# The front of an RWKV-7 / mLSTM / PEER layer: rewritten RWKV preparation, stores issued from ScalarE, w_out interleaved with the merge

## The chip, the cores and the metric

One core of one Trainium2 chip runs the whole layer in one launch. The metric is device time in microseconds (us). PE is the matrix engine (TensorE), DVE is VectorE, ACT is ScalarE, POOL is GpSimd, SP is SyncE, which here does nothing but issue DMAs.

## The reference

One layer on 512 tokens of width 1024, in float32:

```
h = rmsnorm(x);  z = h @ w_in                 # 1024 x 5896
y_rw = rwkv7(z[:, :1792])                     # 8 heads of 64
    zs = z + (z_prev - z) * mu                # token shift, 14 columns of 128
    kk = k*k_k / max(sqrt(sum(k*k_k)^2 per head), 1e-12)
    S = S*w + (S @ -kk) (kk*a)^T + v k^T ;  y = S @ r      # recurrence over tokens
y_ml = mlstm(z[:, 1792:3848])                 # 4 heads of 128, conv of 4 taps
gate = sigmoid(z[:, 3848:] + gate_b)          # two gates of 1024
merged = gate0 * (y_rw @ p_rw) + gate1 * (y_ml @ p_ml)
x1 = x + merged @ w_out
out = rmsnorm(x1 + peer(rmsnorm(x1)))         # product-key experts
```

## The kernel before

All large products are made exact to about float32 by splitting each operand into a high and a low part: `split` (L97 to L99) has ACT copy the high part and DVE or POOL subtract it to get the low part, and `mm3` (L92 to L95) then issues three matmuls (L93, L94, L95) where one would do. A "column" is a block of 128 of w_in's outputs for all 512 tokens: one 512 KB load, one split (`wh` on ACT, `wl` on DVE), 24 matmuls of 128x512 into a PSUM tile `m`. There are 46 columns and one for the mLSTM gates.

The front runs in stages. (1) Prologue: x is normalised in four blocks of 128 tokens (`norm`, L111 to L119: a square with a sum, a reciprocal root, a scaling), transposed on PE (L127) and split into `hh`, `hl`; the first two columns go ahead in halves (`cols2`). (2) Preparation: `shifted` makes the token shift of a column (POOL subtract L217, DVE combine L218); `prep(i)` (L268 to L353) makes for each pair of heads the decay, the normalised key `kk`, the scaled tensors, and three groups of PE work: a norm (L288), the bonus sum (L324, over `rx`), four transposed tensors (L337, copied by ACT at L339 and stored by SP) and 32 small products (L349, L350). (3) Inverse: 31 steps of a DVE multiply and reduce (L393, L395) invert 32x32 blocks for all chunks. (4) Solve: the recurrence over four blocks of 128 tokens (L412 to L521), a chain PE, ACT, DVE, PE. The mLSTM heads (`mhead`) and the remaining columns (`mcol` stores z to `dz`, `gate` stores to `dgate`) fill the gaps of PE. (5) Merge (L640 to L727): 8 "m" branches and 8 "r" branches of 12 matmuls each, then `half(b, 0, ...)`, the first half of w_out for four token blocks, 24 matmuls each. `branch` multiplies the product by the gate on DVE (L680); in an r branch POOL adds the m part (L694) and `split` makes `mh`, `ml`, which w_out needs for all d. (6) From the second half of w_out on (the tile `o`): norm2, the query projection and the PEER experts.

The engines each run their instructions in the order they stand. The order in the front is worked out by the framework's scheduler from the program and the pools' buffer counts; a list F says how many columns are put between the pieces. From (6) on the order is written by hand and every engine's instructions there stand in the same order in both kernels. SP's queue holds the loads and the stores in one row: a store that waits for its producer keeps the loads behind it.

Of the kernel before, what the change touches and what calls it, by code (L numbers as in the profile page):

```python
# [73 lines left out]
def hybrid_block(ctx: ExitStack, tc: tile.TileContext, A, out, dbg=None):  # L74
# [64 lines left out]
    with ExitStack() as fr:  # L139
# [16 lines left out]
        with ExitStack() as st:  # L156
            xp = pool(st, "xp", 2)
            for b in range(TB):
                xt = xp.tile([128, D], FT, name="xt", bufs=4)
                nc.sync.dma_start(xt, A["x"][b * 128:(b + 1) * 128, :])  # L160
                if b == 0:
                    nc.sync.dma_start(ident, A["ident"])
                    nc.sync.dma_start(vec, A["vec"])
                xs = norm(xp, xt)
                transposed(xp, sm, xs, "norm1_g", hh, hl, b, (b % 2,))

        def wtile(src, n, sub=None):
            w = wr.tile([128, KD, n], FT, name="wf")
            nc.sync.dma_start(w, src)
            h = wr.tile([128, KD, n], FR, name="wh")  # L170
            l = wr.tile([128, KD, n], FR, name="wl")
            split(w, h, l, sub)
            return h, l

# [11 lines left out]
        def cols2(j0):  # L186

            ws = [wtile(A["w_in_t"][j], 128, nc.gpsimd) for j in (j0, j0 + 1)]
# [11 lines left out]
        first = cols2(12)  # L200
# [7 lines left out]
        zwa = tmp.tile([128, T], FT, name="zwa")  # L208
        def shifted(j, dst, ps=None):
# [22 lines left out]
        def gate(j):  # L232
# [3 lines left out]
            nc.sync.dma_start(dgate[j], t)  # L236
# [5 lines left out]
        def mcol(n):  # L242
# [4 lines left out]
            nc.sync.dma_start(dz[4 * j + h], t)  # L247
# [24 lines left out]
        def prep(i):  # L272
# [30 lines left out]
            nc.gpsimd.tensor_tensor(L, L, sg, op=OP.subtract)  # L303
# [10 lines left out]
            nc.gpsimd.tensor_tensor(bh, kk, aa, op=OP.mult)  # L314
# [16 lines left out]
            nc.gpsimd.tensor_tensor(v8(bp), v8(bh), pcb, op=OP.mult)  # L331
            nc.gpsimd.tensor_tensor(v8(kp), v8(kh), pcb, op=OP.mult)
            for n, src in enumerate((vx, None, bp, kp)):
# [6 lines left out]
                nc.sync.dma_start(dX[:, :, n, i * 128:(i + 1) * 128].rearrange("b p c -> p b c"), tt)  # L340
# [303 lines left out]
    mp = pool(me, "mp1", 1, side="right", reuse_waits="tile")  # L644
    mf = [mp.tile([128, T], FT, name=f"mf{d}") for d in range(KD)]
    ysm = [mp.tile([128, 4, T], FR, name="ym" + x) for x in "hl"]
    mt = pool(me, "mt", 2, side="right", reuse_waits="tile")
# [34 lines left out]

    todo = [("m", A["p_ml_t"][d], 8 + d) for d in range(KD)] + [("r", A["p_rw_t"][d], d) for d in range(KD)]
    ahead = [weights(*todo.pop(0))]
    load_y("m", dym)
    for d in range(2 * KD):
# [11 lines left out]

    def wo_tiles(c, his, los):

        for k in range(KD):
            w = mt.tile([128, 512], FT, name="wo", bufs=2)
            nc.sync.dma_start(w, A["w_out"][k * 128:(k + 1) * 128, c * 512:(c + 1) * 512])
            split(w, his[k], los[k])
        return list(zip(his, los))

    def half(b, c, wo, ps, part):

        sl, cs = slice(b * 128, (b + 1) * 128), slice(c * 512, (c + 1) * 512)
        for k in range(KD):  # L710
            mm3(ps, mh[:, k, sl], ml[:, k, sl], wo[k][0], wo[k][1], k == 0, k == KD - 1)
        nc.vector.tensor_tensor(xts[b][:, cs], xts[b][:, cs], ps, op=OP.add)
        sc = mt.tile([128, 512], FT, name="sc", tag="pg", bufs=3)
        nc.scalar.activation(sc, xts[b][:, cs], AF.Square, accum_out=part)

    sq = [[mq.tile([128, 1], FT, name=f"sq{b}{c}") for c in range(2)] for b in range(TB)]
    wo = wo_tiles(0, [m3.tile([128, 512], FR, name=f"woh{k}") for k in range(KD)],
                  [m3.tile([128, 512], FR, name=f"wol{k}") for k in range(KD)])
    for b in range(TB):
        nc.sync.dma_start(xts[b], A["x"][b * 128:(b + 1) * 128, :])  # L720
        half(b, 0, wo, mm.tile([128, T], FT, name="m"), sq[b][0])
    wl = [mp.tile([128, 4, 512], FR, name=f"wol1{n}", tag="ym" + "hl"[n]) for n in range(2)]
    wo = wo_tiles(1, [mp.tile([128, 512], FR, name=f"woh1{k}", tag=f"mf{k}") for k in range(KD)],
                  [wl[k // 4][:, k % 4] for k in range(KD)])
    me2.close()

# [87 lines left out]
    transposed(mt, rps, xs[3], "norm2_g", th, tl, 3)  # L814
# [547 lines left out]
```

## Time and profile before

| what | us |
|---|---|
| median of 3 runs | 1925.1 (1921.32 to 1927.17) |
| the profiled execution, its own time | 1927.14 |
| span of its trace | 1925.4 |
| prologue, 0 to 40.2 | PE busy 21.39 |
| preparation, 40.2 to 236.3 | PE busy 177.55 of 196.10 |
| inverse, 236.3 to 305.7 | PE busy 62.23 of 69.40 |
| solve, 305.7 to 479.8 | PE busy 172.85 of 174.10 |
| merge, 479.8 to 565.9 | PE busy 73.19 of 86.10 |
| the rest, 565.9 to the end | PE busy 1312.19 of 1359.50 |

The span is cut at the first and last matmuls of the stages. Busy is the sum of the time in which an engine had an instruction running; PEclk in a row is the clock that TensorE was granted, as a share of 2.4 GHz.

### The profile page before, as it was taken

How to read it: one execution, taken by the hardware profiler on the slowest of the kernel's cores; microseconds unless marked ns; L12 is line 12 of the kernel's file. 1: busy time of each engine (PE TensorE's matmuls, PEld its weight loads, DVE VectorE, ACT ScalarE, POOL GpSimd, SP SyncE). 2: the span in 40 equal slices, each digit the busy share in tenths (PEclk: the TensorE clock that was granted, in tenths of full speed). 3: DMA queues.
4: the chain of work that ended last, by engine and by line, in shares of the span. 5: the costliest groups of instructions: out<-in, count | busy, mean ns of one | idle time of the engine just before them, and what ended most of it. 6: DMA issues, size and time to landing. Idle time of an engine off the chain costs nothing.

```text
span 1925.4 us, 27329 instructions
## 1 busy us (share of the span) xinstructions
PE 1819.4 (94%) x10241; PEld 1593.6 (83%) x10241; DVE 1386.7 (72%) x2516; ACT 743.0 (39%) x1099; POOL 619.3 (32%) x538
## 2 busy tenths in 40 slices
PE   6888999999889998998999999999999999999998
PEld 5666777888668988897999977799999999998786
DVE  4568693544634599989888556777788878787975
ACT  4346432654434333323444433333333333333433
POOL 2421102110123555453222211144554444443400
PEclk8989999999999999998999999999999999999999
DMA  3244645432834344344888988989999999998982
GB/s 141 83 139 156 170 154 199 146 107 88 280 112 151 123 162 153 110 160 140 269 265 266 290 289 276 309 299 319 327 330 314 337 312 338 314 328 274 370 279 84
DMA packets 242499, 431.37 MB, mean 224 GB/s; under 512 B 22976, under 2 KB 149568, under 8 KB 241344
## 3 DMA queue, kind: packets, MB, share of 16 engines
q1 hardware_dynamic: 156144, 270.24, 42.2%
q0 software_dynamic: 36864, 134.23, 20.1%
q10 hardware_dynamic: 49360, 25.17, 4.7%
q8 instruction: 80, 1.31, 0.3%
q14 instruction: 51, 0.42, 0.1%
HBM read 372.83 MB, written 56.75 MB: 223 GB/s over the span
## 4 chain that ended last, share of the span: by engine, by line
PE 67%; DVE 17%; DMA 7%; issue 4%; ACT 3%; POOL 2%; SPq 0%; DVEq 0%; ACTq 0%; POOLq 0%
PE h L93 7%; PE h L94 7%; PE h L95 7%; PE po L93 7%; PE po L94 7%; PE po L95 7%; PE w L1163 5%; PE m L95 3%; PE m L93 3%; DMA as<-dA 3%; PE m L94 3%; DVE wl L99 1%; DVE vl L99 1%; DMA vf<-in_v_dram 1%; DVE ge L1006 1%
## 5 line engine op out<-in xcount | busy, mean ns | idle before, releaser
L93 PE MATMUL h<-tl,wh 128*128 128x384 f32 x1024 | 350.8, 343 | 0.0
L95 PE MATMUL h<-th,wl 128*128 128x384 f32 x1024 | 347.3, 339 | 3.2 <-POOL wl L99 3.2
L94 PE MATMUL h<-th,wh 128*128 128x384 f32 x1024 | 347.2, 339 | 0.0
L859 POOL DMA_INDIRECT gat<-in_u_dram,eid x128 | 176.1, 1376 | 404.1 <-DVE gat L864 387.5
L93 PE MATMUL po<-vl,ah 128*128 128x512 f32 x654 | 258.8, 396 | 14.7 <-DVE vl L99 14.5
L94 PE MATMUL po<-vh,ah 128*128 128x512 f32 x654 | 257.5, 394 | 0.0
L95 PE MATMUL po<-vh,al 128*128 128x512 f32 x654 | 257.2, 393 | 0.0
L98 ACT ACTIVATE wh<-wf 128x1024 fp32r<-128x1024 f32 x208 | 218.6, 1053 | 90.8 <-PE m L94 58.5
L859 POOL DMA_INDIRECT gat<-in_v_dram,eid x128 | 180.8, 1412 | 215.8 <-DVE acc L870 190.2
L99 DVE TENSOR_TENSOR vl<-vf,vh 128x1024 fp32r<-128x1024 f32 x111 | 135.9, 1224 | 131.0 <-ACT vh L98 130.8
L99 DVE TENSOR_TENSOR wl<-wf,wh 128x1024 fp32r<-128x1024 f32 x152 | 188.0, 1237 | 50.7 <-ACT wh L98 48.7
L854 ACT ACTIVATE act<-h 128x384 f32<-128x384 f32 x98 | 48.2, 492 | 429.9 <-PE h L95 429.9
L95 PEld LDWEIGHTS h<-th,wl 128*128 128x128 f32 x1024 | 195.4, 191 | 3.5 <-POOL wl L99 3.5
L93 PEld LDWEIGHTS h<-tl,wh 128*128 128x128 f32 x1024 | 196.3, 192 | 2.4
L94 PEld LDWEIGHTS h<-th,wh 128*128 128x128 f32 x1024 | 195.8, 191 | 2.3
L99 POOL TENSOR_TENSOR wl<-wf,wh 128x1024 fp32r<-128x1024 f32 x56 | 136.5, 2448 | 142.8 <-ACT wh L98 140.3
L870 DVE SCALAR_TENSOR_TENSOR acc<-gat,dots,acc 128x1024 f32<-128x1024 f32 x128 | 164.0, 1281 | 2.4
L864 DVE SCALAR_TENSOR_TENSOR gat<-gat,tok 128x1024 f32<-128x1024 f32 x128 | 159.2, 1267 | 4.0 <-DMA gat<-in_u_dram,eid 4.0
L93 PE MATMUL m<-hl,wh 128*128 128x512 f32 (+1 forms) x392 | 155.1, 396 | 5.6 <-ACT wh L98 5.6
L95 PE MATMUL m<-hh,wl 128*128 128x512 f32 (+1 forms) x392 | 154.9, 395 | 5.1 <-DVE wl L99 4.9
L93 PEld LDWEIGHTS po<-vl,ah 128*128 128x128 f32 x654 | 124.5, 190 | 41.8 <-ACT ah L98 17.2
L94 PE MATMUL m<-hh,wh 128*128 128x512 f32 (+1 forms) x392 | 153.9, 393 | 0.0
(384 smaller groups left out, 3344.4 us busy)
## 6 DMA issues: line engine op xcount, KB each, us to landing
wf<-in_u_t_dram SPq DMA_DIRECT2D x128, 512.0 KB
vf<-in_v_dram SPq DMA_DIRECT2D x111, 512.0 KB
W<-dW SPq DMA_DIRECT2D x32, 768.0 KB
wf<-in_w_in_t_dram SPq DMA_DIRECT2D x46, 512.0 KB
dW<-stg ACTq DMA_DIRECT2D x11, 2048.0 KB
wf<-in_v_dram SPq DMA_DIRECT2D x17, 512.0 KB
wf<-in_w_q_t_dram SPq DMA_DIRECT2D x16, 512.0 KB
dA<-as SPq DMA_DIRECT2D x30, 192.0 KB
```

What stands on the lines that cost most here:

```text
L93: nc.tensor.matmul(ps, lh, rl, start=first, stop=False)
L94: nc.tensor.matmul(ps, lh, rh, start=False, stop=False)
L95: nc.tensor.matmul(ps, ll, rh, start=False, stop=last)
L98: nc.scalar.activation(hi, src, AF.Copy)
L99: (sub or nc.vector).tensor_tensor(lo, src, hi.bitcast(FT), op=OP.subtract)
L854: nc.scalar.activation(act[i], ps, AF.Gelu)
L859: nc.gpsimd.indirect_dma_start(out=t, out_offset=None, in_=src, in_offset=bass.IndirectOffsetOnAxis(ap=eid[:, j:j + 1], axis=0))
L864: nc.vector.scalar_tensor_tensor(t, t, 1.0, tok0, op0=OP.mult, op1=OP.mult, accum_out=dots[:, j:j + 1])
L870: nc.vector.scalar_tensor_tensor(acc, t, dots[:, j:j + 1], acc, op0=OP.mult, op1=OP.add)
L1006: nc.vector.tensor_tensor(ge, x.rearrange("p b (a r) -> p (b a) r", r=4).unsqueeze(2).to_broadcast(big), rank.unsqueeze(1).to_broadcast(bi ...
L1163: nc.tensor.matmul(ps[:, r], og[k][:, a, :, r], O1[:, a, :, r], start=k == 0, stop=k == 1)
```

## The change

1. Prologue: the square with its sum goes from ACT to DVE; the four x loads and the loads of the first two weight tiles are issued together, x0 and x1 before the weights, x2 and x3 behind them; all low parts are made by DVE.
2. `shifted`: z*(1-mu) is made by ACT, DVE adds z_prev*mu. POOL's subtract goes.
3. `prep`: the sum of squares is made by four matmuls with the tokens on the partitions (2 columns each), so that the root, the reciprocal and the Newton step work on 128x8 instead of 128x512; the result is spread out to 128x512 and put back by four PE transposes (L310 of the changed kernel). L-sg, bh, bp and kp go from POOL to DVE.
4. The stores of `dgate`, `dz` and `dX` (16 each) are issued from ACT's queue.
5. Merge: weights are fetched two branches ahead; x and the w_out tiles are loaded and split within the loop over the r branches, four tiles deep instead of two; the first half of w_out is computed tile by tile (`first_half(k)`: 12 matmuls, tile k for four token blocks) two r branches behind the branch that made its input, into four PSUM tiles of their own.

```diff
-        nc.scalar.activation(xs, xt, AF.Square, accum_out=ss)
+        nc.vector.scalar_tensor_tensor(xs, xt, 1.0, xt, op0=OP.mult, op1=OP.mult, accum_out=ss)
...
-            d = tmp.tile([128, T], FT, name="zd", bufs=2)
-            nc.gpsimd.tensor_tensor(d, z[:, 0:T], z[:, 1:], op=OP.subtract)
-            nc.vector.scalar_tensor_tensor(dst, d, V("rw_mu", j), z[:, 1:], op0=OP.mult, op1=OP.add)
+            nc.scalar.activation(dst, z[:, 1:], AF.Identity, scale=omu[:, j:j + 1])
+            nc.vector.scalar_tensor_tensor(dst, z[:, 0:T], V("rw_mu", j), dst, op0=OP.mult, op1=OP.add)
...
-            nc.sync.dma_start(dgate[j], t)
+            nc.scalar.dma_start(dgate[j], t)
...
-            ps = sm.tile([128, T], FT, name="s")
-            nc.tensor.matmul(ps, C("bdones"), q, start=True, stop=True)
-            nc.scalar.activation(q, ps, AF.Sqrt)
-            nc.vector.tensor_scalar(q, q, 1e-19, None, op0=OP.max)
-            nc.vector.reciprocal(q, q)
+            ps = sm.tile([128, TB, 2], FT, name="s")
+            for tb in range(TB):
+                nc.tensor.matmul(ps[:, tb], q[:, tb * 128:(tb + 1) * 128], C("bdones")[:, 0:128:64], start=True, stop=True)
+            n2 = tmp.tile([128, TB, 2], FT, name="n2", bufs=2)
+            nc.vector.tensor_copy(n2, ps)
+            iv = tmp.tile([128, TB, 2], FT, name="iv", bufs=2)
+            nc.scalar.activation(iv, n2, AF.Sqrt)
+            nc.vector.tensor_scalar(iv, iv, 1e-19, None, op0=OP.max)
+            nc.vector.reciprocal(iv, iv)
+            nc.vector.scalar_tensor_tensor(n2, iv, -0.5, n2, op0=OP.mult, op1=OP.mult)
+            nc.vector.tensor_tensor(n2, n2, iv, op=OP.mult)
+            nc.vector.scalar_tensor_tensor(iv, n2, 1.5, iv, op0=OP.add, op1=OP.mult)
+            ivb = tmp.tile([128, TB, 2, 64], FT, name="ivb")
+            nc.vector.tensor_scalar(ivb, iv.unsqueeze(3).to_broadcast([128, TB, 2, 64]), 1e12, None, op0=OP.min)
+            ps = sm.tile([128, TB, 128], FT, name="s")
+            for tb in range(TB):
+                nc.tensor.transpose(ps[:, tb], ivb[:, tb], ident)
+            nc.vector.tensor_tensor(kk, kk, ps.rearrange("p b t -> p (b t)"), op=OP.mult)
             L = tmp.tile([128, T], FT, name="L")
-            nc.vector.scalar_tensor_tensor(L, q, -0.5, ps, op0=OP.mult, op1=OP.mult)
-            nc.gpsimd.tensor_tensor(L, L, q, op=OP.mult)
-            nc.vector.scalar_tensor_tensor(q, L, 1.5, q, op0=OP.add, op1=OP.mult)
-            nc.vector.scalar_tensor_tensor(kk, q, 1e12, kk, op0=OP.min, op1=OP.mult)
...
-            nc.gpsimd.tensor_tensor(bh, kk, aa, op=OP.mult)
+            nc.vector.tensor_tensor(bh, kk, aa, op=OP.mult)
...
+    def first_half(k):
+
+        for b in range(TB):
+            sl = slice(b * 128, (b + 1) * 128)
+            mm3(pso[b], mh[:, k, sl], ml[:, k, sl], wo[k][0], wo[k][1], k == 0, k == KD - 1)
+
     todo = [("m", A["p_ml_t"][d], 8 + d) for d in range(KD)] + [("r", A["p_rw_t"][d], d) for d in range(KD)]
-    ahead = [weights(*todo.pop(0))]
+    LAG = 2
     load_y("m", dym)
+    ahead = [weights(*todo.pop(0)), weights(*todo.pop(0))]
...
+            wo.append(wo_tile(0, d, m3.tile([128, 512], FR, name=f"woh{d}"), m3.tile([128, 512], FR, name=f"wol{d}")))
+            if d < TB:
+                nc.sync.dma_start(xts[d], A["x"][d * 128:(d + 1) * 128, :])
+            if d >= LAG:
+                first_half(d - LAG)
+    for k in range(KD - LAG, KD):
+        first_half(k)
```

How instructions move, in three places. First DVE in the preparation of the first pair of heads, ahead of the bonus sum's input `rx`; before:

```order
L310 TENSOR_TENSOR KR<-rx,ei 128x512
L315 TENSOR_TENSOR bh<-bh,en 128x512
L320 TENSOR_TENSOR kh<-kx,en 128x512
L322 SCALAR_TENSOR_TENSOR rx<-rx,vec,kx 128x512
L309 TENSOR_TENSOR KR<-kk,L 128x512
```

and in the changed kernel, where L338 makes `rx` and L311 waits for the four transposes:

```order
L307 TENSOR_SCALAR ivb<-iv 128x512
L323 COPY PC<-ei 128x8
L326 TENSOR_TENSOR KR<-rx,ei 128x512
L311 TENSOR_TENSOR kk<-kk,s 128x512
L319 TENSOR_TENSOR L<-L,sg 128x512
L330 TENSOR_TENSOR bh<-kk,aa 128x512
L99 TENSOR_TENSOR wl<-wf,wh 128x1024
L325 TENSOR_TENSOR KR<-kk,L 128x512
L331 TENSOR_TENSOR bh<-bh,en 128x512
L333 TENSOR_SCALAR aa<-aa,vec 128x512
L347 TENSOR_TENSOR bp<-bh,PC 128x512
L334 SCALAR_TENSOR_TENSOR kx<-aa,kx 128x512
```

L-sg, bh and bp now stand in DVE's row; `rx` follows two rows later.

Second SP's queue where the merge's loads begin (`yl` loads the mLSTM's output, `pw` a branch's weights, `pg` its gate); before:

```order
L236 DMA dgate_360<-ze_4016 128x512
L667 DMA pw_4104<-in_p_ml_t_dram 128x512
L669 DMA pg_4106<-dgate_360 128x512
L662 DMA yl_4112<-dym_63 128x512
L662 DMA yl_4116<-dym_63 128x512
L662 DMA yl_4120<-dym_63 128x512
L236 DMA dgate_360<-ze_4050 128x512
L662 DMA yl_4124<-dym_63 128x512
```

and after:

```order
L636 DMA dym_63<-so_3283 128x512
L158 DMA wf_4059<-in_w_in_t_dram 128x1024
L679 DMA yl_4159<-dym_63 128x512
L537 DMA dyr_62<-ya_3711 512x1x128
L679 DMA yl_4163<-dym_63 128x512
L679 DMA yl_4167<-dym_63 128x512
L679 DMA yl_4171<-dym_63 128x512
L686 DMA pg_4177<-dgate_360 128x512
```

The gate stores have left the row (they stand in ACT's), and the `yl` loads stand ahead of the weights and the gates.

Third PE where the third r branch ends; in the changed kernel the first w_out tile follows (`wo0` to `wo3` are the four PSUM tiles), and then the fourth r branch:

```order
L95 MATMUL m_4455<-yrh_4139,pwl_4388 128x512
L93 MATMUL wo0_4155<-wol0_4409,mh_4118 128x512
L94 MATMUL wo0_4155<-woh0_4408,mh_4118 128x512
L95 MATMUL wo0_4155<-woh0_4408,ml_4119 128x512
L93 MATMUL wo1_4156<-wol0_4409,mh_4118 128x512
L94 MATMUL wo1_4156<-woh0_4408,mh_4118 128x512
L95 MATMUL wo1_4156<-woh0_4408,ml_4119 128x512
```

Before, the first matmul on `mh` stood behind the last r branch:

```order
L94 MATMUL m_4495<-yrh_4099,pwh_4474 128x512
L95 MATMUL m_4495<-yrh_4099,pwl_4475 128x512
L93 MATMUL m_4569<-wol0_4528,mh_4094 128x512
L94 MATMUL m_4569<-woh0_4520,mh_4094 128x512
L95 MATMUL m_4569<-woh0_4520,ml_4095 128x512
```

Twelve matmuls of w_out now stand between two r branches from the third on, and 24 behind the last.

## Rows read from the trace of the kernel before

**Rows 1.** Windows by stage: start:end, us, each engine's busy us, PEclk, DMA share, GB/s

```profile
0.00:40.20 40.20, 21.39 (x128) 20.38 (x129) 20.31 (x37) 15.62 (x26) 12.14 (x16) 0.87 0.40 142
40.20:236.30 196.10, 177.55 (x943) 135.41 (x942) 131.16 (x154) 99.99 (x133) 53.93 (x52) 0.96 0.46 139
236.30:305.70 69.40, 62.23 (x260) 49.08 (x259) 58.12 (x86) 22.77 (x27) 6.91 (x11) 0.98 0.51 172
305.70:479.80 174.10, 172.85 (x1721) 145.56 (x1721) 77.42 (x172) 83.46 (x134) 20.14 (x26) 1.00 0.37 122
479.80:565.90 86.10, 73.19 (x289) 55.99 (x289) 46.08 (x67) 31.51 (x55) 12.82 (x9) 0.94 0.62 202
565.90:1925.40 1359.50, 1312.19 (x6906) 1187.22 (x6904) 1053.60 (x2001) 489.62 (x724) 513.33 (x425) 0.98 0.76 256
```

**Rows 2.** Waits of PE from 0 to 580: total us, times, longest

```profile
PE s L324 <- DVE rx L322: 16.2, 4, 5.7
PE s L127 <- DVE xs L118: 14.7, 2, 12.5
...
PE m L93 <- ACT mh L98: 5.6, 2, 3.1
...
PE m L93 <- DVE yml L99: 3.9, 2, 3.6
```

**Rows 3.** Timeline of DVE, prologue: start, us, instruction

```profile
20.70 2.08 DVE L107 TENSOR_TENSOR rsq<-rs 128x1 f32<-128x1 f32 x1
```

**Rows 4.** Page, costliest groups: count, busy us, mean ns

```profile
L99 DVE TENSOR_TENSOR wl<-wf,wh 128x1024 fp32r<-128x1024 f32 x152 | 188.0, 1237 | 50.7 <-ACT wh L98 48.7
...
L864 DVE SCALAR_TENSOR_TENSOR gat<-gat,tok 128x1024 f32<-128x1024 f32 x128 | 159.2, 1267 | 4.0 <-DMA gat<-in_u_dram,eid 4.0
```

**Rows 5.** Timeline of DVE, first preparation

```profile
77.97 3.35 DVE L291 RECIPROCAL q<-q 128x512 f32<-128x512 f32 x1
...
84.36 1.52 DVE L295 SCALAR_TENSOR_TENSOR q<-L,q 128x512 f32<-128x512 f32 x1 [1.18 <-POOL L L294]
...
88.86 0.49 DVE L317 TENSOR_SCALAR aa<-aa,vec 128x512 f32<-128x512 f32 x1 [1.12 <-POOL bh L314]
...
93.19 0.68 DVE L320 TENSOR_TENSOR kh<-kx,en 128x512 f32<-128x512 f32 x1
93.80 1.52 DVE L322 SCALAR_TENSOR_TENSOR rx<-rx,vec,kx 128x512 f32<-128x512 f32 x1
```

**Rows 6.** Timeline of PE, first preparation

```profile
95.38 2.08 PE L324 MATMUL s<-rx,cst 128*128 128x512 f32 x2 [5.67 <-DVE rx L322]
```

**Rows 7.** Windows of two stretches with the lower granted clock

```profile
94.16:100.98 6.82, 5.61 (x20) 4.14 (x22) 6.16 (x7) 1.19 (x2) 2.26 (x4) 0.50 0.27 77
...
544.71:551.54 6.83, 5.24 (x12) 4.13 (x13) 2.60 (x5) 3.13 (x6) 1.07 (x2) 0.50 0.36 111
```

**Rows 8.** Timeline of PE, merge

```profile
508.90 0.39 PE L93 MATMUL m<-yml,pwh 128*128 128x512 f32 x1
509.13 0.40 PE L94 MATMUL m<-ymh,pwh 128*128 128x512 f32 x1
...
546.30 0.80 PE L93 MATMUL m<-wol,mh 128*128 128x512 f32 x1 [3.08 <-ACT mh L98]
```

**Rows 9.** Timeline of POOL, merge

```profile
535.96 1.61 POOL L694 TENSOR_TENSOR pg<-pg,mf 128x512 f32<-128x512 f32 x1 [2.13 <-DVE pg L680]
539.70 1.58 POOL L694 TENSOR_TENSOR pg<-pg,mf 128x512 f32<-128x512 f32 x1 [2.13 <-DVE pg L680]
```

**Rows 10.** Transfers from 479 to 520: packets, MB, mean GB/s

```profile
DMA packets 6241, 11.82 MB, mean 288 GB/s; under 512 B 690, under 2 KB 690, under 8 KB 6238
```

**Rows 11.** Timeline of SP's queue, start of the merge

```profile
481.33 0.32 SPq L236 DMA_DIRECT2D dgate<-ze  x1
481.74 0.38 SPq L662 DMA_DIRECT2D yl<-dym  x1
```

**Rows 12.** Stores issued from ACT: ns min/median/max

```profile
L1169 ACTq DMA_DIRECT2D dW<-stg x13: 366/366/868, 914.1 to 1089.5; - x13
```

More of the change, by code (lines that the diff above doesn't have):

```diff
@@ L155, in hybrid_block @@
         hl = io.tile([128, KD, T], FR, name="hl")
[L156 to L165, printed above, removed]
         def wtile(src, n, sub=None):
@@ L173, in wtile @@
             return h, l
+        with ExitStack() as st:
+            xp = pool(st, "xp", 2)
+            xt = []
+            for b in range(TB):
+                xt.append(xp.tile([128, D], FT, name="xt", bufs=4))
+                nc.sync.dma_start(xt[b], A["x"][b * 128:(b + 1) * 128, :])
+                if b == 0:
+                    nc.sync.dma_start(ident, A["ident"])
+                if b == 1:
+                    nc.sync.dma_start(vec, A["vec"])
+                    ws12 = [wtile(A["w_in_t"][j], 128) for j in (12, 13)]
+            for b in range(TB):
+                xs = norm(xp, xt[b])
+                transposed(xp, sm, xs, "norm1_g", hh, hl, b)
         def col(j):
@@ L184, in colw, with cols2 @@
             return ps
-        def cols2(j0):
-            ws = [wtile(A["w_in_t"][j], 128, nc.gpsimd) for j in (j0, j0 + 1)]
+        def cols2(ws):
             ps = [mm.tile([128, T], FT, name="m") for _ in range(2)]
@@ L199, in hybrid_block @@
         zg = rw.tile([128, T], FT, name="zg")
-        first = cols2(12)
+        first = cols2(ws12)
         nc.sync.dma_start(cst, A["cst"])
@@ L208, in hybrid_block @@
         zwa = tmp.tile([128, T], FT, name="zwa")
+        omu = tmp.tile([128, 14], FT, name="omu")
+        o_mu = VEC["rw_mu"][0]
+        nc.vector.tensor_scalar(omu, vec[:, o_mu:o_mu + 14], -1.0, 1.0, op0=OP.mult, op1=OP.add)
         def shifted(j, dst, ps=None):
@@ L643, in hybrid_block @@
     me = ExitStack()
[L644 to L647, printed above, removed]
     mq = pool(me, "mp", 1, side="right", reuse_waits="tile")
@@ L651, in hybrid_block @@
     ml = mq.tile([128, KD, T], FR, name="ml")
+    mp = pool(me, "mp1", 1, side="right", reuse_waits="tile")
+    ysm = [mp.tile([128, 4, T], FR, name="ym" + x) for x in "hl"]
+    mt = pool(me, "mt", 2, side="right", reuse_waits="tile")
+    mf = [mp.tile([128, T], FT, name=f"mf{d}") for d in range(KD)]
     me2 = ExitStack()
@@ L655, in hybrid_block @@
     mm = pool(me2, "mm2", 4, space=PSUM, reuse_waits="tile")
+    wps = pool(me2, "wo2", 1, space=PSUM, reuse_waits="tile")
     ys = {}
@@ L681, in branch, with wo_tile, residual, half @@
         return dst
+    def wo_tile(c, k, hi, lo):
+        w = mt.tile([128, 512], FT, name="wo", bufs=4)
+        nc.sync.dma_start(w, A["w_out"][k * 128:(k + 1) * 128, c * 512:(c + 1) * 512])
+        split(w, hi, lo)
+        return hi, lo
+    def residual(b, c, ps, part):
+        cs = slice(c * 512, (c + 1) * 512)
+        nc.vector.tensor_tensor(xts[b][:, cs], xts[b][:, cs], ps, op=OP.add)
+        sc = mt.tile([128, 512], FT, name="sc", tag="pg", bufs=3)
+        nc.scalar.activation(sc, xts[b][:, cs], AF.Square, accum_out=part)
+    def half(b, c, wo, ps, part):
+        sl = slice(b * 128, (b + 1) * 128)
+        for k in range(KD):
+            mm3(ps, mh[:, k, sl], ml[:, k, sl], wo[k][0], wo[k][1], k == 0, k == KD - 1)
+        residual(b, c, ps, part)
+    sq = [[mq.tile([128, 1], FT, name=f"sq{b}{c}") for c in range(2)] for b in range(TB)]
+    pso = [wps.tile([128, 512], FT, name=f"wo{b}") for b in range(TB)]
+    wo = []
+    def first_half(k):
+        for b in range(TB):
+            sl = slice(b * 128, (b + 1) * 128)
+            mm3(pso[b], mh[:, k, sl], ml[:, k, sl], wo[k][0], wo[k][1], k == 0, k == KD - 1)
     todo = [("m", A["p_ml_t"][d], 8 + d) for d in range(KD)] + [("r", A["p_rw_t"][d], d) for d in range(KD)]
-    ahead = [weights(*todo.pop(0))]
+    LAG = 2
     load_y("m", dym)
+    ahead = [weights(*todo.pop(0)), weights(*todo.pop(0))]
     for d in range(2 * KD):
@@ L697, in hybrid_block @@
             split(t, mh[:, d], ml[:, d])
[L699 to L718, printed above, removed]
+            wo.append(wo_tile(0, d, m3.tile([128, 512], FR, name=f"woh{d}"), m3.tile([128, 512], FR, name=f"wol{d}")))
[5 more added lines that the diff above has]
+        first_half(k)
     for b in range(TB):
-        nc.sync.dma_start(xts[b], A["x"][b * 128:(b + 1) * 128, :])
-        half(b, 0, wo, mm.tile([128, T], FT, name="m"), sq[b][0])
+        residual(b, 0, pso[b], sq[b][0])
     wl = [mp.tile([128, 4, 512], FR, name=f"wol1{n}", tag="ym" + "hl"[n]) for n in range(2)]
-    wo = wo_tiles(1, [mp.tile([128, 512], FR, name=f"woh1{k}", tag=f"mf{k}") for k in range(KD)],
-                  [wl[k // 4][:, k % 4] for k in range(KD)])
+    wo = [wo_tile(1, k, mp.tile([128, 512], FR, name=f"woh1{k}", tag=f"mf{k}"), wl[k // 4][:, k % 4])
+          for k in range(KD)]
     me2.close()
+    mn = pool(me, "mn", 2, side="right", reuse_waits="tile")
     NS = 128
```

18 lines of the change are left out of this document (9 added, 9 removed).

## The prediction

> **What bounds the kernel now.** I first cut the span by stage [rows 1]. The reader should compare PE's busy time with each stretch: PE is busy 1819 of 1925 us, so a change pays only where PE idles or runs at its lower clock. From 565.9 on both kernels have the same instructions in the same order on every engine, so those 1359.5 us stay. Ahead of that PE is idle for 18.8 us in the prologue, 18.6 in the preparation, 7.2 in the inverse, 1.3 in the solve and 12.9 in the merge: 58.7 us in all, the most that better cover could give beside the clock.
>
> Next, what ended PE's waits [rows 2]. In the preparation nearly all of them, 16.2 of 18.6 us, are one wait, four times over: the bonus sum's matmul L324 for `rx`, the last product of a long DVE chain. In the prologue it is the normalised x (14.7 of 18.8). In the merge there are two: 5.6 for `mh`, and 3.9 for `yml` at its start.
>
> Then the clock. The chain's wait costs twice: in the first preparation PE idled 5.67 us before L324 [rows 6] and the granted clock stood at 0.50, which is 1.2 GHz, for 6.82 us around it [rows 7]. The preparation has three such spells, 17.1 us together, and the merge has two, 10.3 us.
>
> **The change part by part.**
>
> *Prologue.* Four squares leave ACT and come to DVE; the nearest row for a multiply with a sum over 1024 columns took 1.27 us [rows 4], so DVE gains 5 us of work. In return POOL no longer subtracts there. A DVE instruction on 128x1 took 2.08 us while POOL was splitting a weight tile [rows 3], and it is the first of three stretched ones, 5.6 us together, where the first block's counterparts ran unstretched beside an idle POOL. The Trainium skill has the reason on its page "SBUF — State Buffer" (SBUF: two separate sides): DVE and POOL share a port pair that one of them locks for a whole instruction. By it the three stretched instructions vanish wholly, as I assume; if the stretch had another source, the prologue would gain nothing. Against the gain, x2 and x3 now stand behind two weight tiles: 1 MB at 288 GB/s [rows 10] is an estimated 3.6 us later. Bounds -5 (all of the stretch goes) and +3.5; I take -2.5, since the first halves of the columns need x0 and x1 alone and the weights are earlier by as much.
>
> *Preparation.* Removed from DVE's chain: the 3.35 us reciprocal, the 1.52 us Newton product, and two waits for POOL, 1.18 and 1.12 us [rows 5]. Four 512-wide passes come to DVE from POOL; a clean pass takes 0.68 and one beside a POOL pass 1.52 [rows 5], and with POOL left almost without work I take 0.68. The small chain is some six instructions of a few columns, bounded by 0.1 us and by the stretched 2.08 each [rows 3]; I take 0.2. What matters to PE is the cover in its own row. A column's matmuls start 0.23 us apart [rows 8]. In the first preparation of the changed kernel 19 of them (4.4 us) stand between the small matmuls and the transposes, and 35 (8.1 us) between the transposes and the bonus sum. DVE has for the second stretch ten passes of about 0.68 and one split of 1.24 [rows 4, 5], 8.0 us: even. For the first it has the scan, the small chain, a spread to 512 columns and ACT's root with a table change: some 4.5 us, again even. So the 16.2 us go, and with them the three clock spells: PE was busy for 5.61 of the 6.82 us shown [rows 7], so half of that, 2.8, and 7 over the three. New waits at the transposes and at the later copies and products, up to 1 us each time, take 2 back. This gives -21. Bounds: -25 (a little also from the shorter wait for PSUM) and -10 (the passes stay at 1.52 us: ten passes lose 8.4 us, less what slack is left; half of the waits and the clock stay).
>
> The moved stores: `dX`, `dz`, `dgate` go one by one from SP's row to ACT's, each behind the ACT instruction that made its data, so none adds a wait; each costs ACT 0.37 us, 0.87 at the most [rows 12]. Behind them on ACT stand the next column's `wh` copies. ACT is busy 100 of 196 us in the preparation [rows 1], and 16 to 20 issues there are 6 us: hidden. If that cover went, it would cost those 6 us.
>
> *Inverse.* DVE bounds it: busy 58.1 of 69.4 us [rows 1]. The preparation ends some 10 us earlier against the columns, so more of the mLSTM's convolution and one more split fall between the inverse's steps on DVE, and the solve starts later after them: +2, bounds 0 and +5.
>
> *Solve.* PE is full [rows 1], because columns fill the recurrence. With columns used up earlier about 220 instead of 244 column matmuls are left to interleave before the last block's end; 24 x 0.23 = 5.5 us of cover is gone, and ten gate stores on ACT stand in the recurrence's row, 10 x 0.37 = 3.7 us. Bounds 0 and +8 (more than either alone, less than both); I take +3, as columns that aren't used as cover still run behind.
>
> *Merge.* Its work is 288 matmuls at 0.23 us, 66.3 us of 86.1. Today the r branches run in a loop of 3.74 us: the DVE product, POOL's add (1.61 us, starts 3.74 apart [rows 9]), ACT's copy, DVE's subtract; a branch is only 12 x 0.23 = 2.8 us on PE. So `mh` is late, PE waits twice for it in w_out (5.6 us [rows 2], the second 3.08 [rows 8]), and runs 6.8 us at 1.2 GHz [rows 7]. With 12 w_out matmuls between two branches a round on PE is 5.5 us, longer than the loop; both waits and that spell go. The `yml` wait (3.9) and its spell go too if the loads stand early: a `dgate` store at 481.33 held the fourth `yl` load until 481.74 [rows 11]. Here a rule speaks against the change. The Trainium skill, "DMA: Bandwidth & Descriptors" (Issuing engines are not separate DMA queues), says that issuing from another engine saves only the sequencer's issue time. By it the store's move would save 0.3 us and the `yml` wait would stay: 1896 instead of 1892. The row shows something else, a load held by order, so I keep the gain. The sum of what could go is 12.9 idle and 4.2 of clock (half of 8.5 busy), 17.1; I leave 2 for a transfer that is late at the first r branch: -15, bounds -17 and -8.
>
> Sum: -2.5 - 21 + 2 + 3 - 15 = -33.5. The profiled execution took 1927.1, so 1893.6; the median of the runs lies 2.0 lower: **1892**.
>
> **The rivals.**
>
> *A: the preparation gives it back.* PE now has two hand-overs to DVE in each preparation instead of one and a half. If DVE's inherited passes run slow, half of the preparation's saving stays away (-10), and the inverse and the solve take their upper parts (+5, +6): -16.5, so 1909. For it: DVE was busy for 131 of 196 us already [rows 1]. Against it: the stretched rows stand beside POOL work that is now gone.
>
> *B: the merge is bound by its loads.* Ahead of the first r branch now stand 5 w_out tiles and four x blocks, about 10.5 MB with the rest: at 288 GB/s [rows 10] an estimated 36 us, against 22 us of m branches and some 16 of last columns. If the lead isn't there, up to 14 us of wait at the first r branch take the merge's gain: 1906. For it: the DMAs ran at that rate through the whole stretch. Against it: the loads of weights don't wait for the recurrence.
>
> *C: slower, ScalarE.* ACT runs in order, and 48 stores are now among its copies. If each holds the recurrence, or the `wh` copy that PE waits for next, for the longest time seen, 48 x 0.87 = 42 us come on top: 1934. It decides from 33.5/48 = 0.70 us per store on the path. Against it: the median is 0.37, and ACT is busy for less than half of the solve [rows 1].
>
> *D: nothing.* PE's waits only change their names, as every chain is as long as before: 1925. Against it: the reciprocal and the POOL waits leave the chain without a substitute of their size.
>
> **How the numbers follow.** Forecast 0.63, A 0.20, B 0.10, C 0.04, D 0.03. The forecast's own bounds are 1881 to 1903. The range of 1878 to 1912 takes in A and B, which lie on the same side, and leaves out C and D and the far bounds. About 0.3% (6 us) is what a measurement of this kernel can tell: faster 0.92 (forecast, A and B, less a little of A's tail), same 0.04, slower 0.04.
>
> **What would show it.** Right: L340's wait (the bonus sum) below 1 us each time, no half-clock stretch around it; no wait for `mh` in the merge and one half-clock spell there at most; the stage from the first `o` matmul to the end 1359 us as before; the merge near 70 us, the stretch up to the solve near 285. Wrong: a wait of 2 us or more at the transposes for `ivb` (A); PE waiting for `yrl` or `pwh` at the first r branch (B); ACT issue time ahead of `wh`, or of the recurrence's copies, as the releaser of PE (C); a solve above 182 us would break the sum most.

## The result, and the profile after

The changed kernel took 1896.9 us (median of 4 runs, 1887.5 to 1902.1) against 1925.4 before (1921.3 to 1927.2): a ratio of 0.9849, 95% interval 0.9807 to 0.9892. In a later comparison with more runs it took 1895.0 against 1926.8, ratio 0.984 [0.9818, 0.9862], which is 31.7 us less. The forecast was 33.5 us less, 1892, with a range of 1878 to 1912. The profiled execution happened to be the shortest of this kernel's, 1887.5 us with a span of 1885.7.

The windows of the changed kernel, cut at the same events as [rows 1] (columns: start:end, us, busy us of PE, PEld, DVE, ACT, POOL, granted clock, DMA share, GB/s):

```profile
0.00:32.50 32.50, 19.19 (x128) 17.86 (x129) 23.34 (x52) 11.32 (x18) 0.52 (x9) 1.00 0.48 176
32.50:207.90 175.40, 168.76 (x964) 131.37 (x962) 104.37 (x172) 101.01 (x142) 2.72 (x16) 0.99 0.49 151
207.90:282.50 74.60, 66.62 (x269) 53.20 (x269) 63.12 (x96) 26.10 (x32) 8.17 (x15) 0.93 0.50 174
282.50:458.60 176.10, 174.89 (x1730) 147.49 (x1729) 82.79 (x179) 82.53 (x137) 17.91 (x25) 1.00 0.40 130
458.60:530.00 71.40, 67.28 (x289) 55.18 (x288) 41.63 (x63) 26.85 (x47) 11.70 (x8) 0.98 0.68 234
530.00:1885.70 1355.70, 1308.40 (x6905) 1185.02 (x6905) 1057.02 (x2001) 490.76 (x728) 518.26 (x425) 0.98 0.76 256
```

The reader should subtract these stage by stage from [rows 1]:

| stage | before | after | difference | forecast |
|---|---|---|---|---|
| prologue | 40.2 | 32.5 | -7.7 | -2.5 |
| preparation | 196.1 | 175.4 | -20.7 | -21 |
| inverse | 69.4 | 74.6 | +5.2 | +2 |
| solve | 174.1 | 176.1 | +2.0 | +3 |
| merge | 86.1 | 71.4 | -14.7 | -15 |
| from `o` on | 1359.5 | 1355.7 | -3.8 | 0 |

Up to `o` PE's busy time fell from 507.2 to 496.7 us and its idle time from 58.7 to 33.3. The time at 1.2 GHz fell from 41.0 us (eight spells) to 17.1 (four; 27.3 in a later profile of the same kernel). The clock is the part that the waits' table doesn't show.

PE's waits from 0 to 560, in answer to [rows 2] (total us, times, longest):

```profile
PE m L95 <- DVE wl L99: 9.3, 4, 3.7
PE s L127 <- DVE xs L118: 8.8, 1, 8.8
PE m L93 <- DVE hl L99: 4.2, 1, 4.2
PE m L93 <- ACT ze L241: 4.1, 1, 4.1
PE s L365 <- ACT tt L355: 2.7, 3, 1.1
```

The bonus sum (now L340) and the transposes (L310) are absent from the answer, and so is `mh`. What is new is a wait of 4.1 us at the merge's start for a gate's sigmoid, `ze`; the largest sum is now the low parts of columns' weights, 7.8 us of it in the inverse.

The chain on DVE in the first preparation, in answer to [rows 5] (start, us, instruction):

```profile
70.01 0.17 DVE L301 TENSOR_SCALAR iv<-iv 128x8 f32<-128x8 f32 x1 [0.65 <-ACT iv L300]
70.22 0.20 DVE L302 RECIPROCAL iv<-iv 128x8 f32<-128x8 f32 x1
...
71.06 0.43 DVE L307 TENSOR_SCALAR ivb<-iv 128x512 f32<-128x512 f32 x1
...
73.84 0.69 DVE L330 TENSOR_TENSOR bh<-kk,aa 128x512 f32<-128x512 f32 x1
...
77.17 0.69 DVE L347 TENSOR_TENSOR bp<-bh,PC 128x512 f32<-128x512 f32 x1
...
79.10 0.74 DVE L338 SCALAR_TENSOR_TENSOR rx<-rx,vec,kx 128x512 f32<-128x512 f32 x1
```

From the clamp after the root to the end of `rx` it takes 9.8 us (70.01 to 79.84), where it took 17.8 (77.51 to 95.32). The reciprocal went from 3.35 to 0.20 us, and every pass that came from POOL takes 0.69.

### The profile page after: what moved, and what is told of

Same layout as the page of the kernel before. It is cut to its first block, busy times and chain, and to the rows that moved or that the text cites. A ratio compares the mean times of both kernels' runs of the same rounds, so it can differ in the third digit from the quotient of the medians.

```text
span 1885.7 us, 27396 instructions
## 1 busy us (share of the span) xinstructions
PE 1805.1 (96%) x10281; PEld 1590.1 (84%) x10281; DVE 1372.3 (73%) x2559; ACT 738.6 (39%) x1099; POOL 559.3 (30%) x498
## 4 chain that ended last, share of the span: by engine, by line
PE 59%; DVE 11%; DMA 4%; issue 1%; ACT 1%; POOL 1%; SPq 0%; DVEq 0%; ACTq 0%; POOLq 0%
PE po L93 8%; PE h L93 8%; PE h L95 8%; PE h L94 8%; PE po L94 8%; PE po L95 8%; PE w L1197 5%; DMA as<-dA 2%; PE m L95 1%; PE m L93 1%; PE m L94 1%; DVE vl L99 1%; DMA vf<-in_v_dram 1%; DVE mr L1001 1%; DVE gat L898 1%
## 5 line engine op out<-in xcount | busy, mean ns | idle before, releaser
L893 POOL DMA_INDIRECT gat<-in_v_dram,eid x128 | 186.4, 1456 | 209.6 <-DVE acc L904 184.0
L93 PEld LDWEIGHTS h<-tl,wh 128*128 128x128 f32 x1024 | 196.1, 192 | 2.4
```

The source lines that it names most:

```text
L93: nc.tensor.matmul(ps, lh, rl, start=first, stop=False)
L893: nc.gpsimd.indirect_dma_start(out=t, out_offset=None, in_=src, in_offset=bass.IndirectOffsetOnAxis(ap=eid[:, j:j + 1], axis=0))
```

## The experiments

Each profile is compared by the start of its first 512-token column matmul (prologue), the first step of the inverse, the last column's matmul and the first `o` matmul. In the changed kernel these are 32.5, 207.9, 458.3 and 530.05 us. Each edit has one profile, so its difference counts only beyond what the profiles scatter: over ten profiles of kernels with the changed prologue its end lies between 32.3 and 33.7.

**The changed kernel again** (no edit).

> The changed kernel itself, once more. The front (up to the first `o` matmul) is fixed by order and waits, so it should end at 530 us again, within 1 us, and the prologue (first column matmul over 512 tokens) at 32.5. If instead the spread of the changed kernel's runs (1887 to 1902) arises in the front, `o` will start elsewhere, up to 15 us later. My theory: the spread arises behind `o`, in the stretches of lower granted clock and waits of the PEER part; the length behind `o` will differ from 1355.7 us by several us.

It took 1895.7 us. The prologue ended at 33.1 and `o` started at 530.85; from there to the end it took 1363.1 us instead of 1355.6. So of the 8.3 us between these two profiles, 7.5 arose behind `o`: PE was idle there for 57.6 us instead of 47.2, and its time at 1.2 GHz was shorter (43.5 instead of 46.2), so waits made the difference, not the clock.

**Squares of the prologue on ACT.**

```diff
-        nc.vector.scalar_tensor_tensor(xs, xt, 1.0, xt, op0=OP.mult, op1=OP.mult, accum_out=ss)
+        nc.scalar.activation(xs, xt, AF.Square, accum_out=ss)
```

> The four squares of the prologue back on ScalarE, all else as changed. Theory: the prologue gained 7.7 us instead of the 2.5 forecast because ScalarE no longer changes its table between the squares and the roots and the first block's root is not behind the second block's square; then the first transposes move from 8.8 to 10.5 or later and the first 512-token column matmul from 32.5 to 34 to 36. Rival: VectorE, busy without a gap from 14 to 27 us, is what bounds the changed prologue; then taking 5 us of squares from it makes it end at 30 or earlier.

The first transposes moved from 8.8 to 11.3 us and the prologue ended at 35.45, 2.9 later. ACT's timeline of this run shows why:

```profile
7.04 1.06 ACT L115 ACTIVATE xs<-xt 128x1024 f32<-128x1024 f32 x1 [1.38 <-DMA xt<-in_x_dram]
8.01 0.19 ACT L115 ACTIVATION_READ_ACCUMULATOR xs<-xt 128x1 f32 x1
8.21 1.28 ACT L104 ACT_TABLE_LOAD   x1
9.50 0.29 ACT L104 ACTIVATE rs<-ss 128x1 f32<-128x1 f32 x2
```

The root stands behind the second block's square and a table change of 1.28 us. That VectorE's squares bound the prologue is refuted: without them it took 24.1 us from the first transposes on, 23.8 with them.

**Parameter vectors ahead of x1.**

```diff
                 if b == 0:
                     nc.sync.dma_start(ident, A["ident"])
-                if b == 1:
                     nc.sync.dma_start(vec, A["vec"])
+                if b == 1:
                     ws12 = [wtile(A["w_in_t"][j], 128) for j in (12, 13)]
```

> The load of the parameter vectors (60 KB in short rows) stands ahead of x1 again, all else as changed. Theory: x1 then lands 2 to 2.5 us later, as before the change (8.2 us), the first root stands behind x1's square on VectorE, so the first transposes start near 11 and the column matmuls at 512 tokens at 34 to 35. Rival: the order of these small loads is hidden; 32.5 as in the changed kernel.

The first transposes started at 10.1 and the prologue ended at 35.1, 2.6 later. On DVE the second block's square started at 7.32 instead of 5.99, so x1 was 1.3 us late rather than the 2 to 2.5 expected; the direction and the end are as the theory had them.

**Low parts of the prologue on POOL.**

```diff
-                    ws12 = [wtile(A["w_in_t"][j], 128) for j in (12, 13)]
+                    ws12 = [wtile(A["w_in_t"][j], 128, nc.gpsimd) for j in (12, 13)]
...
-                transposed(xp, sm, xs, "norm1_g", hh, hl, b)
+                transposed(xp, sm, xs, "norm1_g", hh, hl, b, (b % 2,))
```

> The low parts of the prologue on GpSimd where they stood there before the change (two weight tiles, every second half block), all else as changed. Theory of the prediction: VectorE's small instructions are stretched again to 1 to 2.3 us beside them and the prologue ends at 35 to 38. Rival: VectorE has less to do, the stretch is small, and the prologue ends at 32.5 or earlier.

The prologue ended at 38.0, 5.5 later and within the theory's numbers, by a stretch of DVE, but of other instructions than the theory names. DVE's timeline of this run:

```profile
9.66 2.86 DVE L118 TENSOR_SCALAR xs<-xt,rs 128x1024 f32<-128x1024 f32 x1
...
13.65 2.17 DVE L115 SCALAR_TENSOR_TENSOR xs<-xt 128x1024 f32<-128x1024 f32 x1
...
19.81 1.74 DVE L99 TENSOR_TENSOR hl<-hf,hh 128x512 fp32r<-128x512 f32 x1
...
21.66 0.16 DVE L107 TENSOR_TENSOR rsq<-rs 128x1 f32<-128x1 f32 x1
```

and POOL's:

```profile
9.62 5.12 POOL L99 TENSOR_TENSOR wl<-wf,wh 128x1024 fp32r<-128x1024 f32 x2 [8.71 <-ACT wh L98]
14.70 2.24 POOL L99 TENSOR_TENSOR hl<-hf,hh 128x512 fp32r<-128x512 f32 x1
19.43 1.57 POOL L99 TENSOR_TENSOR hl<-hf,hh 128x512 fp32r<-128x512 f32 x1 [2.48 <-ACT hh L98]
25.76 1.27 POOL L99 TENSOR_TENSOR hl<-hf,hh 128x512 fp32r<-128x512 f32 x1 [4.76 <-ACT hh L98]
```

The small instructions of 0.16 us settle nothing: the roots' passes all ran with POOL idle (ahead of its first split at 9.62, at 18.61, or between 21.00 and 25.76). What ran beside a split was stretched: a scaling took 2.86 us instead of 0.75, a square 2.17 instead of 1.22, and two low parts (one at 15.75) 1.74 instead of 0.69, 5.2 us in all on DVE. POOL's low parts of 128x512 took 2.24 and 1.57 us beside them and 1.27 with DVE mostly idle. The first column matmul started at 21.7 instead of 17.2.

**Passes of the preparation back on POOL.**

```diff
-            nc.vector.tensor_tensor(L, L, sg, op=OP.subtract)
+            nc.gpsimd.tensor_tensor(L, L, sg, op=OP.subtract)
...
-            nc.vector.tensor_tensor(bh, kk, aa, op=OP.mult)
+            nc.gpsimd.tensor_tensor(bh, kk, aa, op=OP.mult)
...
-            nc.vector.tensor_tensor(v8(bp), v8(bh), pcb, op=OP.mult)
-            nc.vector.tensor_tensor(v8(kp), v8(kh), pcb, op=OP.mult)
+            nc.gpsimd.tensor_tensor(v8(bp), v8(bh), pcb, op=OP.mult)
+            nc.gpsimd.tensor_tensor(v8(kp), v8(kh), pcb, op=OP.mult)
```

> L-sg, bh, bp and kp of the preparation back on GpSimd, the small norm chain kept. The preparation took 175.4 us in the changed kernel (first 512-token column to the inverse's first step). Theory 1 (the moved passes matter as much as the norm): VectorE's passes beside GpSimd's take 1.2 to 1.5 us again and the chain waits for GpSimd twice, so PE waits 2 to 4 us at the bonus sum each time with its lower clock: 185 to 192 us. Theory 2 (the norm alone did it): the chain is shorter by 7 us than before the change and fits under the columns: 175 to 178.

**The 512-wide norm back** (from the matmul on `bdones` to the product that makes `kk`).

```diff
-            ps = sm.tile([128, TB, 2], FT, name="s")
...
+            nc.tensor.matmul(ps, C("bdones"), q, start=True, stop=True)
+            nc.scalar.activation(q, ps, AF.Sqrt)
+            nc.vector.tensor_scalar(q, q, 1e-19, None, op0=OP.max)
+            nc.vector.reciprocal(q, q)
...
+            nc.vector.scalar_tensor_tensor(kk, q, 1e12, kk, op0=OP.min, op1=OP.mult)
```

> The 512-wide norm chain back (one matmul, root, 3.35 us reciprocal, Newton passes, one of them on GpSimd), the other passes kept on VectorE. Theory 1 of the run before: half of the gain stays, the preparation takes 183 to 188 us. Theory 2 (the norm alone did it): nearly all of the gain goes, 190 to 196 us.

By stage, passes back on POOL (preparation, inverse, solve):

```profile
33.70:216.30 182.60, 171.03 (x940) 131.00 (x938) 100.10 (x155) 98.84 (x138) 24.86 (x32) 0.96 0.45 138
216.30:291.30 75.00, 66.55 (x269) 53.38 (x269) 64.76 (x96) 26.56 (x32) 7.62 (x14) 0.93 0.52 179
291.30:476.10 184.80, 183.53 (x1753) 154.30 (x1753) 84.32 (x181) 84.69 (x140) 18.84 (x27) 0.98 0.42 135
```

and the old norm:

```profile
32.70:226.40 193.70, 180.67 (x972) 138.32 (x970) 125.35 (x171) 111.02 (x149) 8.74 (x22) 0.97 0.47 143
226.40:294.50 68.10, 60.09 (x245) 48.02 (x246) 59.40 (x86) 24.71 (x28) 7.27 (x12) 0.92 0.54 185
294.50:468.00 173.50, 172.30 (x1705) 145.32 (x1705) 77.91 (x173) 78.10 (x130) 18.97 (x27) 0.98 0.37 119
```

Read by the preparation alone, 182.7 lies below theory 1 and 193.6 would say "the norm did it". Both readings mislead, and so did my measure: the scheduler moves columns between the stages. The preparation holds 547 column matmuls before the change, 528 after, 504 with the passes on POOL and 576 with the old norm. What can be compared is the whole stretch from the first 512-token column to the last one, which holds the same columns in every kernel: 439.2 us before, 425.8 after, 442.2 with the passes on POOL, 435.1 with the old norm. The changed kernel's own three profiles scatter from 425.8 to 430.4 there. Neither part alone gives the gain: both together gave 13.4 us (8.8 against the slowest of the three), and taking one back loses 16.4 (11.9) with the passes or 9.3 (4.7) with the norm. But neither brought back more than 2 of the 16.2 us that PE waited at the bonus sum. PE's waits, first with the passes on POOL, then with the old norm:

```profile
PE s L340 <- DVE rx L338: 1.1, 2, 0.6
```

```profile
PE m L93 <- ACT wh L98: 8.1, 1, 8.1
...
PE s L331 <- DVE rx L329: 1.9, 2, 1.7
```

The 16.4 us of the passes are 5.5 of idle time in small pieces, 17 us more at 1.2 GHz (worth up to 8.5), and 2 that I can't place. With the old norm most is one wait of 8.1 us for a column's high part at the start of the inverse (1.2 us in the changed kernel): its load stood in SP's row behind loads of the inverse's input, which took SP from 207.7 to 223.7. That comes from where the scheduler put the loads, not from the norm's chain, so what each part is worth on that chain stays open. The new form of `shifted` was not taken back alone.

**Stores on SP.**

```diff
-            nc.scalar.dma_start(dgate[j], t)
+            nc.sync.dma_start(dgate[j], t)
...
-            nc.scalar.dma_start(dz[4 * j + h], t)
+            nc.sync.dma_start(dz[4 * j + h], t)
...
-                nc.scalar.dma_start(dX[:, :, n, i * 128:(i + 1) * 128].rearrange("b p c -> p b c"), tt)
+                nc.sync.dma_start(dX[:, :, n, i * 128:(i + 1) * 128].rearrange("b p c -> p b c"), tt)
```

> The 48 stores of dgate, dz and dX issued from SP again, all else as changed. Prediction's reading: loads stand behind waiting stores again, so the merge's first matmul waits longer and columns' loads come late; `o` starts 2 to 6 us later than 530. By the rule that only issue time is saved: within 1 us of 530. Against both: ScalarE, free of 48 issues, lets the solve be 1 to 3 us shorter.

`o` started at 533.1, 3.0 later than in the first profile of the changed kernel and 1.8 earlier than in its third (534.9, below). Merge and column stretch, 72.1 and 428.0 us, also lie among those of the changed kernel (71.7 to 72.2, 425.8 to 430.4). A gain from the moved stores can't be told from none here.

**Merge as before.** The pools, `load_y`, `weights`, the loop and `half` of the kernel before, in the changed front.

```diff
-            wo.append(wo_tile(0, d, m3.tile([128, 512], FR, name=f"woh{d}"), m3.tile([128, 512], FR, name=f"wol{d}")))
...
-            if d >= LAG:
-                first_half(d - LAG)
...
+    for b in range(TB):
+        nc.sync.dma_start(xts[b], A["x"][b * 128:(b + 1) * 128, :])
+        half(b, 0, wo, mm.tile([128, T], FT, name="m"), sq[b][0])
```

> The merge (pools, loads, loops) as before the change, all else as changed. From the last column's matmul to the first `o` matmul it took 86.5 us before and 71.7 after. Theory: the merge's gain is its own, so this run shows 85 to 88 us and `o` at 544 to 546. Rival: part of it came from the stores that left SP's queue or from the earlier front, then 76 to 82.

From the last column's matmul to `o` it took 88.4 us, against 86.5 before the change and 71.7 after (`o` at 549.3). PE's waits there:

```profile
PE m L93 <- ACT mh L98: 5.2, 2, 2.8
PE m L93 <- DVE yml L99: 4.4, 1, 4.4
PE m L93 <- ACT pwh L98: 4.1, 2, 3.8
```

The merge's gain is its own: the two waits of [rows 2] are back, with 17.1 us at the lower clock, and the stores that had left SP's queue didn't shorten the wait for `yml`.

**Banks traded.**

```diff
-    mm = pool(me2, "mm2", 4, space=PSUM, reuse_waits="tile")
     wps = pool(me2, "wo2", 1, space=PSUM, reuse_waits="tile")
+    mm = pool(me2, "mm2", 4, space=PSUM, reuse_waits="tile")
```

> The PSUM pool of the four w_out tiles is opened ahead of the branches' pool, so the two trade banks; nothing else. In the changed kernel PE waits 4.1 us at the merge's first matmul for the last gate's sigmoid, which stands on ScalarE behind the copy of a w_out tile that was still being loaded. Theory: the first branch's PSUM tile lies in the bank which that sigmoid reads; with the banks traded the wait falls below 1.5 us, the half-clock stretch there goes, and `o` starts 4 to 6 us earlier (525 to 527). Rival: PE waits there because a later load or split is late anyway (weights of the first branch), the wait keeps its length under another name, `o` within 1 us of 530.

First the changed kernel, ACT at the merge's start:

```profile
461.52 0.63 ACT L98 ACTIVATE woh<-wo 128x512 fp32r<-128x512 f32 x1 [2.04 <-DMA wo<-in_w_out_dram]
462.06 0.67 ACT L241 ACTIVATE ze<-m,vec 128x512 f32<-128x512 f32 x1
```

The last gate's sigmoid stands behind a w_out copy that waits for its load, and PE's first merge matmul started at 462.78, as the sigmoid ended. With the banks traded that wait is gone (0.0 us) and so is the half-clock spell in the merge; the m branches end 4.2 us earlier against the last column (the first r branch starts 23.7 us behind it, in the changed kernel 28.0). But PE now waits later; PE's waits of this run behind 180 us:

```profile
PE m L93 <- ACT pwh L98: 2.1, 3, 1.4
...
PE m L93 <- DVE yrl L99: 0.8, 2, 0.5
```

The bank was the cause of the wait: in this run too the sigmoid stood behind a w_out copy and ran at 464.75, and no matmul waited for it. Of the 4.1 us only 1.1 were kept (merge 70.6 after 71.7); `o` started at 531.8, since the front ahead of the merge was 2.9 longer in this execution.

**Splits in the inverse on POOL.**

```diff
             for _ in range(n):
                 if others:
+                    SUB[0] = nc.gpsimd if 10 <= 33 - len(others) < 20 else None
                     others.pop(0)()
+                    SUB[0] = None
...
-            h, l = wtile(src, 128)
+            h, l = wtile(src, 128, SUB[0])
```

> The splits of the ten columns that fall into the inverse make their low parts on GpSimd instead of VectorE, all else as changed. The inverse took 74.6 us (73.6 the second time) with VectorE busy for 63. If VectorE's own work bounds it and the two engines ran freely, 10 x 1.2 us would leave its row: 62 to 66 us. If they hold each other up, as the rows of the preparation show, VectorE's steps lengthen by about as much as they save: 72 to 78, and waits of PE for a low part from GpSimd (2.4 us each) appear.

The inverse took 77.6 us with 220 column matmuls in it instead of 269, and `o` started at 549.0. PE's waits and, behind them, the multiplies of the inverse's steps and the convolution passes on DVE in this run:

```profile
PE m L95 <- POOL wl L99: 18.4, 6, 13.9
```

```profile
L413 DVE TENSOR_TENSOR pr<-TT,As 128x4 f32<-128x4 f32 (+29 forms) x30 | 33.8, 1127 | 0.7
...
L582 DVE SCALAR_TENSOR_TENSOR acc<-cz,vec,acc 128x512 f32<-128x512 f32 x15 | 15.4, 1025 | 0.0
```

In the changed kernel the multiplies took 24.2 us in all and a convolution pass 0.75 on average, so beside POOL's splits they lengthened by 9.6 and 4.1 us, about what the twelve low parts that left DVE in this stage had taken (1.22 each). The rival holds for DVE: the engines lengthen each other's work. PE's long wait, 13.9 of the 18.4 us, is something else: that column's load was issued at 272.56, behind the store of the inverse's result in SP's row, and ACT waited 13.7 us for it; POOL's split was only the last 3.3. So 549.0 overstates what the splits cost.

**x later, banks traded**, and **the changed kernel in five rounds**.

```diff
-            if d < TB:
-                nc.sync.dma_start(xts[d], A["x"][d * 128:(d + 1) * 128, :])
+            if d >= TB:
+                nc.sync.dma_start(xts[d - TB], A["x"][(d - TB) * 128:(d - TB + 1) * 128, :])
```

> The banks traded as in the run before, and the x blocks loaded with the fifth to eighth r branch instead of the first to fourth. With the banks traded alone the merge's first wait went (4.1 us), but 2.8 us came back as waits for the splits of `pw` and `yl` around the first r branch, and the merge was only 1.2 us shorter. If those waits are transfers queued behind the x blocks, moving two of the four blocks behind them takes 1.5 to 2.8 us more, the merge is 67.5 to 69 us and `o` 2.5 to 4 us ahead of the changed kernel. If they are ScalarE's order (copies of w_out tiles ahead of the branch's own), nothing changes: 70 to 71 us. On the clock of the whole kernel either is within what the runs scatter.

> The changed kernel in five rounds beside the run before. The front ends within 1 us of 530 again; the length behind `o` (1355.6 and 1363.1 so far) scatters. If the part behind `o` is on average longer than before the change, the median lies 4 to 8 us above the 1892 forecast, at 1893 to 1900; if the first profile's short part is typical, at 1888 to 1892.

With x later the merge took 70.3 us and PE waited 2.8 us in it, both as with the banks alone: the transfers of x were not what those waits were for, and ScalarE's order is left as the reading, not shown. The time is 1894.1 us (ratio 0.9823 [0.9798, 0.9848]), not to be told from the changed kernel's 1895.0. The changed kernel's own third profile is worth more:

```profile
32.30:212.50 180.20, 173.51 (x964) 135.04 (x962) 104.40 (x173) 101.10 (x142) 2.71 (x16) 0.96 0.48 147
...
534.90:1893.30 1358.40, 1304.78 (x6905) 1181.00 (x6905) 1059.32 (x2001) 490.93 (x727) 507.89 (x425) 0.99 0.76 255
```

The preparation took 4.8 us longer than in the first profile (180.2 against 175.4) with the same instructions and the same 6.7 us of idle time; PE's busy time is longer by as much, and the time at 1.2 GHz is 13.7 us instead of 3.4. My expectation that the front ends within 1 us of 530 failed: it ended at 534.9.

## Why the prediction was right, and where not

The total holds (1895 to 1897 against 1892, 28 to 32 us less against 33.5). The two large terms hold to 0.3 us in the first profile, the shortest run; in the third, near the median (1893.3), the prologue is 5.4 us better than forecast and the preparation 5.1 worse. That these cancel is luck. The forecast's own bounds, 1881 to 1903, are narrower than the sum of its terms' bounds (-47 to -1.5, so 1878 to 1924), and it gives no reason for that.

*Prologue, -2.5 forecast, -7.7 measured: mis-sized, beyond its own bound.* What failed is a term that the sum left out: PE's first wait for the normalised x, 12.5 us long in [rows 2]. It is 8.8 us after the change, so 3.8 of the 7.7 us lie ahead of the first transposes: the root no longer stands behind a second square and a table change of 1.28 us, and x1 no longer behind the short rows of the parameter vectors (2.9 and 2.6 us when undone alone; they overlap). The other 3.9 lie behind the first transposes, where the term that I did have applies: the prologue took 27.7 us from there before, 23.8 after, and 28.6 with the low parts back on POOL. So POOL's splits cost about what I gave the stretch as its upper bound, 5, though by wide passes and their own length; the stretch of 128x1 instructions [rows 3] was not seen again. The cost that I set against it, x2 and x3 behind two weight tiles, did not show.

*Preparation, -21: the waits as forecast, the size partly luck.* The waits at the bonus sum are gone as computed, cover and chain are even as counted, and the passes take 0.69 us as assumed. The small chain took 0.17 to 0.20 us an instruction; I took 0.2. Which of the edits took the waits away isn't shown, since taking back either of two did not bring them back. And 19 of the 547 column matmuls (4.4 us at 0.23) left the stage and came back in the inverse and the solve. Counted so, the preparation gained 16 and the inverse and solve together lost 3, not 7. The sum of the three is -13.5; I had -16. The clock's part of the forecast, 7 us, is the least certain: the same kernel had 3.4 us of half clock in this stage, or 13.7, and with the latter the stage gained 15.9 instead of 20.7.

*Inverse, +2 forecast, +5.2 measured: just beyond its bound of +5.* The mechanism is as forecast, DVE's row filled with convolution passes and splits (63.1 us busy, 58.1 before), and PE waits 7.8 us there for the low parts. The size is off: I counted one split more, and there are two, with 15 convolution passes instead of 9.

*Solve, +3 forecast, +2.0 measured: right by luck.* PE idled 1.2 us in it before and after, so neither the lost cover nor the issues of the stores showed. The 2.0 us are 8 more column matmuls (1.8 us at 0.23), which came from the preparation.

*Merge, -15 forecast, -14.7 measured.* Both `mh` waits and their spell are gone because 12 matmuls stand between branches; undoing the merge's edits costs 17 us. One step failed: the wait at the merge's start did not go, it only changed hands, from `yml` to a sigmoid held behind a w_out copy on ScalarE (3.9 to 4.1 us, and a spell of 3.4 us each time). What I left for a late transfer (2 us) came out here, at another place. It is ScalarE's order, as in rival C, but a copy held PE and not a store: with the stores back on SP a wait of 2.5 us for the sigmoid stayed.

*The stores.* The Trainium skill's rule ("DMA: Bandwidth & Descriptors", Issuing engines are not separate DMA queues) that I weighed and set aside was the better guide: with the stores back on SP the time is the same within the scatter. The loads held by order on SP were real [rows 11], but the wait behind them stayed when they moved (4.4 us for `yml` with the merge as before). That the rule's time of 1896 also fits proves little, as 4 us are within the runs' scatter.

*Port pair.* The Trainium skill's page "SBUF — State Buffer" (SBUF: two separate sides) is borne out for passes with two tensors in SBUF: 1.02 us instead of 0.75 in the inverse, 1.74 instead of 0.69 in the prologue, beside POOL's splits. For the 128x1 instructions no later run shows it, since none of the roots' passes stood beside a split there.

*From `o` on, 0 forecast.* The order is the same, the time is not: 1355.7, 1363.1 and 1358.4 us in three profiles of the changed kernel, 1359.5 in the one of before. So the first profile's -3.8 is scatter.

*Rivals.* A half came true: the inverse gave back its upper bound, the preparation gave nothing back. B did not: no wait for `yrl` or `pwh` at the first r branch until the wait ahead of it was taken away. D is refuted by [rows 2] and the waits after.

## What to carry to other kernels

Where a scheduler places filler work, judge an edit over the whole stretch that holds the same filler, since a stage's length changes with what was put in it. Where a wait on a chain is removed, look at what stands ahead of the next release on the engine that makes it: in the merge a wait of the same length took its place, and when trading two PSUM pools removed that, all but 1.1 of its 4.1 us came back as waits further on. Where an edit is taken back to test a chain, look whether that chain's wait comes back: here the old norm lost 9.3 us, 8.1 of them at a load that the scheduler had put elsewhere, and 1.9 at the wait that it was to test.

## What was not expected of the hardware

The granted clock differs between executions of the same program where waits and order don't: 3.4 or 13.7 us at 1.2 GHz in the same preparation, with 6.7 us of idle time in both, worth 4.8 us. The part behind `o` scatters too (1355.7 to 1363.1 in three profiles), there by idle time. The three spans go from 1885.7 to 1894.0 us; the run of 1902 has no profile, so its cause is open.
